# Loads in the order K, Q, V, one octet's Q in five uneven transfers, and a last store in two halves: a linear attention kernel on one core

## The chip, the cores and the metric

The kernel runs on one core of one Trainium2 chip. The time is device microseconds from one launch, as the median of three runs; before the change it is 125.52 us (125.49 to 125.57). The core's work is shared by TensorE (PE in the profile; its weight loads are PEld), VectorE (DVE), ScalarE (ACT), GpSimd (POOL) and SyncE (SP), and by 16 DMA engines that move data between the device memory and the core's SBUF. GpSimd and SyncE issue all transfers here: GpSimd's go through the queue that the profile calls q0 (software_dynamic), SyncE's through q1 (hardware_dynamic).

## The reference

```python
Q_feat = np.maximum(0, Q); K_feat = np.maximum(0, K)      # (8, 12, 512, 64) each
KV    = np.einsum('bhkd,bhkv->bhdv', K_feat, V)
K_sum = np.sum(K_feat, axis=2)
numerator   = np.einsum('bhqd,bhdv->bhqv', Q_feat, KV)
denominator = np.einsum('bhqd,bhd->bhq', Q_feat, K_sum)
out = numerator / (denominator[:, :, :, None] + 1e-10)    # float32
```

There are 96 heads of 512 rows of 64 numbers. For each head a 64 by 64 matrix KV and a vector of 64 sums come from K and V; each row of Q is then multiplied with them. Q, K and V are 12.58 MB each in float32, and so is the output.

## The kernel before, in words

The 96 heads are worked off in 12 octets of eight heads. An octet of Q, K, V or of the output is 1 MB of device memory, seen as 128 rows of 8 KB: row p lies on partition p of a tile, 2048 numbers long. GpSimd's loads change float32 to bfloat16 on the way, so a load reads 1 MB and writes 0.5 MB.

Python code records the order of all instructions. `do.op` (line 58) records one instruction for an engine, works out from what it reads and writes which semaphores it has to wait for, and gives it one to raise. For a transfer this semaphore is a "lane": GpSimd's transfers take six lanes in turn (`LANES`, line 120), and a transfer also waits for the earlier one of its own lane, so at most six of GpSimd's are under way. An engine takes its instructions strictly in the recorded order; a transfer raises its semaphore by 16 when its last part has landed.

The order of the transfers:

- K and V of octet 0 come through SyncE as float32 into two of the seven output tiles `o_sb` (`NOUT`, line 119); Q of octet 0 comes through GpSimd.
- Octets 1 to 9 are loaded ahead (`AHEAD`, line 117) by `load(o)` (line 179): K, V, then Q. Nine tiles each of `q_sb`, `k_sb` and `v_sb` hold them. Octets 10 and 11 are loaded by `step` after the stores of octets 0 and 1, which GpSimd issues too. The last octet, 11, has K, Q, V.
- The stores of octets 2 to 11 (`store`, line 246) are issued by SyncE. All ten list K of octet 11 among what they read (line 253), so the first of them waits until that load has landed; SyncE issues them in order.

The computation, `step(i)` (line 313), is recorded for DVE, ACT and the DMA queues, and runs as a loop over PE in `products` (line 350). For octet i: DVE copies Q (`copy_q`, line 205), PE transposes it into `ps_qt` (line 360) and ACT applies the relu into `qt`; DVE writes relu(K) into `kf` (line 191), DVE and ACT write V into `vo` (lines 200 and 202), PE multiplies the two into `ps_kv` (line 369), ACT moves the result into `kvd` (line 217). Then PE makes the denominators and the eight heads' numerators (line 354), ACT copies these to `ot` (line 225), PE transposes them back into `ps_x` (line 378), and DVE multiplies by the reciprocals (`norm`, line 239, instruction in line 242), in two halves of 16 rows each, into `o_sb` number (o + 2) mod 7. The transposes back, `norm` and `store` of octet o are recorded in step o + 1, between the parts of the next octet. `norm` of octet o writes the tile that `store` of octet o - 7 reads, so it waits until that store has landed: `norm(9)` for `store(2)`, `norm(10)` for `store(3)`, `norm(11)` for `store(4)`.

Of the kernel before, what the change touches and what calls it, by code (L numbers as in the profile page):

```python
# [8 lines left out]
class Order:  # L9
# [45 lines left out]
        for k in writes:  # L55
            self.writer[k], self.readers[k] = (what, n), []

    def op(self, who, make, reads=(), writes=(), sem=None, dma=None, kept=False):
        engine = self.engines[who]
        waits = []  # L60
        assert not self.kept & set(writes)
        if kept:
            self.kept |= set(reads)
        elif dma:
            writes = [*writes, dma]
        todo = self.needs(who, reads, writes)
        while todo:
            x = max(todo, key=lambda y: sum(self.at[y, todo[y]].get(z, 0) >= m for z, m in todo.items()))
            waits.append(self.done[x, todo[x]])
            self.learn(who, x, todo[x])  # L70
            todo = self.needs(who, reads, writes)
        for s, value in waits[:-1]:
            engine.wait_ge(self.sems[s], value)
        made = make(engine)
        if waits:
            s, value = waits[-1]
            made.wait_op(self.sems[s], value, "sem-ge")
        if kept:
            made.then_inc(self.sems[dma], 16)
            self.count[dma] = self.count.get(dma, 0) + 16  # L80
        elif dma:
            made.then_inc(self.sems[dma], 16)
            self.note(who, dma, reads, writes, dma, 16)
        else:
            made.then_inc(self.sems[sem or who], 1)
            self.note(who, who, reads, writes, sem or who, 1)
# [10 lines left out]
def kernel(  # L97
# [8 lines left out]
    B, H, S, D = Q.shape  # L106
    assert D == 64
    P = 128
# [4 lines left out]
    RQ = S * 8 // P  # L113
    U = RQ // 2
    NO = NH // 8
    assert NO * 8 == NH and R == 16 and RQ == 32
    AHEAD = 9
    NI = AHEAD
    NOUT = 7
    LANES = 6  # L120

    fp32 = mybir.dt.float32
    bf16 = mybir.dt.bfloat16
    Act = mybir.ActivationFunctionType
# [2 lines left out]
    sb = ctx.enter_context(tc.tile_pool(name="sb", bufs=1))  # L127
    psum = ctx.enter_context(tc.tile_pool(name="psum", bufs=1, space=bass.MemoryType.PSUM))

    def view(X, f):  # L130
        return X.rearrange("b h s d -> (b h s d)").rearrange("(n p f) -> n p f", p=P, f=f)

    Qr, Kr, Vr, Or = [view(X, RQ * D) for X in (Q, K, V, out)]
# [9 lines left out]
    q2 = sb.tile([P, U, P], bf16, name="q2")  # L143
# [2 lines left out]
    own = sb.tile([P, U, 8, 2], fp32, name="own")  # L146
    den = sb.tile([P, RQ], fp32, name="den")
    rec = sb.tile([P, RQ], fp32, name="rec")
    q_sb = [sb.tile([P, U, P], bf16, name=f"q_sb{i}") for i in range(NI)]
    k_sb = [sb.tile([P, RQ * D], bf16, name=f"k_sb{i}") for i in range(NI)]  # L150
    v_sb = [sb.tile([P, RQ * D], bf16, name=f"v_sb{i}") for i in range(NI)]
    o_sb = [sb.tile([P, RQ, D], fp32, name=f"o_sb{i}") for i in range(NOUT)]
# [3 lines left out]
    ps_x = [psum.tile([P, 1024], fp32, name=f"ps_x{j}") for j in range(2)]  # L156

    names = ["dve", "act", "pool", "pe", "q2", "a0", "d0", "d1", "ev", "t0", "t1", "n0", "n1"]
    lanes = {"pool": [f"gl{i}" for i in range(LANES)], "sp": [f"sl{i}" for i in range(3)], "last": ["el"]}
    sems = {n: tc.alloc_semaphore("s_" + n) for n in names + sum(lanes.values(), [])}  # L160
    turn = {n: 0 for n in lanes}

    def lane(who):
        turn[who] += 1
        return lanes[who][(turn[who] - 1) % len(lanes[who])]

    do = Order(nc, sems)
# [4 lines left out]
        return [(x[o % NI].rearrange("p (r d) -> p r d", d=D), (n, o % NI)) for n, x in (("k", k_sb), ("v", v_sb))]  # L172

    def load_q(o):
        do.op("pool", lambda e: e.dma_start(out=q_sb[o % NI].rearrange("p u f -> p (u f)"), in_=Qr[o],  # L175
                                            single_packet=True),
              writes=[("q", o % NI)], dma=lane("pool"))

    def load(o):
        i = o % NI  # L180
        for n, X, t in (("K", Kr, k_sb), ("V", Vr, v_sb)):
            if n == "V" and o == NO - 1:
                load_q(o)
            do.op("pool", lambda e: e.dma_start(out=t[i], in_=X[o], single_packet=True), writes=[(n.lower(), i)],  # L184
                  dma=lane("pool"))
        if o < NO - 1:
            load_q(o)

    def prep_k(o, s):
        src, key = kv_src(o)[0]  # L190
# [12 lines left out]
        do.op(who, make, reads=[key, ("mask", 1), "vo1"], writes=[("vo", t, j) for j in halves], sem=sem)  # L203

    def copy_q(o):
        do.op("dve", lambda e: e.tensor_copy(q2, q_sb[o % NI]), reads=[("q", o % NI)], writes=["q2"], sem="q2")  # L206

    def relu_q(j):
        do.op("act", lambda e: e.activation(qt[:, j * (U // 2):(j + 1) * (U // 2)], ps_qt[j], Act.Relu),  # L209
              reads=[("pq", j)], writes=[("qt", j)])  # L210
# [3 lines left out]
    def evac_kv():  # L214
        for s in range(2):
            for c in range(2):
                do.op("act", lambda e: e.copy(  # L217
                    kvd[64 * c:64 * c + 64, s:8:2, c * D1:c * D1 + D1].rearrange("p (g t) d -> p g t d", t=2),
                    ps_kv[64 * s:64 * s + 64, :, 0:2 * (D + 2)].rearrange(
                        "p g (t d) -> p g t d", t=2)[:, :, :, c:c + D1]),  # L220
                    reads=[("pk", 0), ("pk", 1)], writes=[("kvd", s, c)], sem="ev" if s + c == 2 else None)
# [21 lines left out]
                                               rec[:, rs].unsqueeze(2).to_broadcast([P, 16, D]), op=Alu.mult),  # L243
              reads=[("x", j), "rec"], writes=[("o", i, j)] if i > 1 else [("o", i, j), ("o", i)], sem=f"n{j}")

    def store(o):
        i = (o + 2) % NOUT
        to, src = Or[o], o_sb[i].rearrange("p r d -> p (r d)")
        keys = [("o", i, h) for h in range(2)]
        if o + AHEAD + 1 < NO:  # L250
            do.op("pool", lambda e: e.dma_start(out=to, in_=src, single_packet=True), reads=keys, dma=lane("pool"))
        else:
            keys.append(("k", (NO - 1) % NI))
            do.op("sp", lambda e: e.dma_start(out=to, in_=src), reads=keys,
                  dma=lane("sp" if o + NOUT < NO else "last"), kept=o + NOUT >= NO)
# [6 lines left out]
    def memset(who, ap, value, key):  # L262
        do.op(who, lambda e: e.memset(ap, value), writes=[key] if isinstance(key, (str, tuple)) else key)  # L263

    def body():
        for c, X in enumerate((Kr, Vr)):
            do.op("sp", lambda e: e.dma_start(out=o_sb[c].rearrange("p r d -> p (r d)"), in_=X[0]),
                  writes=[("o", c)], dma=lane("sp"))
        load_q(0)
        memset("pool", ident, 0.0, "ident")  # L270
        do.op("pool", lambda e: e.affine_select(out=ident, in_=ident, compare_op=Alu.not_equal, fill=1.0, base=0,
                                                pattern=[[-1, P]], channel_multiplier=1),
              reads=["ident"], writes=["ident"])
        ones = vo[:, :, :, 1:D4 - 1]
        memset("pool", ones[:, :, :, 0:D + 2:D1], 0.0, "vo1")
        for h in range(4):
            memset("pool", ones[32 * h:32 * h + 32, :, h % 2, 0:D + 2:D1], 1.0, "vo1")
        for h in range(4):
            for t in range(2):
                memset("pool", mask[32 * h:32 * h + 32, 1, t:t + 1], 1.0 if h % 2 == t else 0.0,  # L280
                       [("m", h, t), ("mask", 1)])
        for o in range(1, AHEAD + 1):
            load(o)
            if o == 1:
                setup()
        for o in range(NO + 1):
            step(o)
        for n in lanes["pool"] + lanes["sp"]:
            nc.gpsimd.wait_ge(sems[n], do.count[n])
        nc.gpsimd.drain()  # L290

# [21 lines left out]
    def step(i):  # L313
        r = i + 1
        more, last = i + 1 < NO, i == NO

        if not last:
            do.looped([("q2", r)], ["q2", "ident"], [("pq", 0)])
            do.looped([], ["q2", "ident"], [("pq", 1)])
            relu_q(0)  # L320
            relu_q(1)
            do.looped([("a0", r), ("d0", r)], KF[0], PK + ["pd"])
            do.looped([("d1", r)], KF[1], PK + ["pd"])
            evac_kv()
            if more:
                prep_v(i + 1, 1, (0,), "act", "a0")
                copy_q(i + 1)
                prep_k(i + 1, 0)
                prep_k(i + 1, 1)
        if i > 0:  # L330
            o = i - 1
            do.looped([("t0", r), ("t1", r)], [*OT, "ident32"], [("x", 0)])
            do.looped([], [*OT, "ident32"], [("x", 1)])
            for j in range(2):
                norm(o, j)
            store(o)
            if o + AHEAD + 1 < NO:
                load(o + AHEAD + 1)
        if not last:
            do.looped([("ev", r)], [*QT, *KVD], ["pd"])  # L340
            denominators()
            for j in range(2):
                do.looped([(f"n{j}", r)], [*QT, *KVD], [("x", j)])
            copy_ot(0, "act")
            copy_ot(1, "act" if more else "dve")
            if more:
                prep_v(i + 1, 0, (0, 1), "dve", "d0")
                prep_v(i + 1, 1, (1,), "dve", "d1")
# [85 lines left out]
```

## Time and profile before

| What | Value |
|---|---|
| median of three runs | 125.52 us |
| the profiled execution | 125.56 us, of which the span from first to last instruction is 123.7 us |
| busy in the span | PE 85.0 us, DVE 82.4, ACT 78.3, POOL 27.6 |
| queue q0 (GpSimd's transfers) | 5184 packets, 75.8% of the 16 DMA engines' span |
| queue q1 (SyncE's transfers) | 1728 packets, 24.7% |
| device memory | 37.75 MB read, 12.58 MB written |

The page gives the span in 40 slices; the row DMA is the mean busy share of the 16 DMA engines in tenths. A query for stretches of time gives the same share for any window. The chain of waits goes back from the last instruction to what released each step. The trace holds two more kinds of records, from which some numbers below are read: each packet's start, duration, size and queue (not the engine that moved it), and the moments at which a transfer's semaphore was raised, 16 for each transfer, one from each DMA engine. A transfer of 128 rows has 144 packets: 128 rows and 16 small ones, of 4 bytes, that raise the semaphore.

### The profile page before, as it was taken

Reading aid. Unit: us, or ns where it says so; the run is one execution under the profiler, and the core shown is the slowest. Engines: PE = TensorE matmul, PEld = TensorE weight load, DVE = VectorE, ACT = ScalarE, POOL = GpSimd, SP = SyncE. Lnnn points to the kernel's source line nnn. Section 1 sums busy time; section 2 is a strip of 40 time slices with the busy share of each in tenths; the row PEclk is TensorE's granted clock in tenths of the full one; section 3 lists DMA queues with packets and bytes.
Section 4 is the critical chain, followed back from the end, with each engine's and each line's share of the span. In section 5 each row is a group of like instructions: output and inputs, shape, how many; then the busy total and the mean of one; then the engine's idle time right before and its main releaser. Section 6 shows DMA issues by size and latency. Waiting matters only on the chain.

```text
span 123.7 us, 3402 instructions
## 1 busy us (share of the span) xinstructions
PE 85.0 (69%) x1440; PEld 73.5 (59%) x1440; DVE 82.4 (67%) x127; ACT 78.3 (63%) x108; POOL 27.6 (22%) x55
## 2 busy tenths in 40 slices
PE   0000097697896979969799697996978918983900
PEld 0000096686794867949589485794856916972900
DVE  1261904769789697895987959869688649067330
ACT  0000762998987889878898788987869736652000
POOL 5795311331131213312421142221000000000000
PEclk9999999999999999999999999999999996897555
DMA  3999999999999999999999999999999999999955
GB/s 69 404 315 222 213 215 212 212 212 212 216 215 215 212 212 212 217 215 213 213 215 212 212 212 267 334 215 234 354 217 212 404 424 432 421 421 429 434 238 212
DMA packets 6916, 32.55 MB, mean 263 GB/s; under 512 B 768, under 2 KB 768, under 8 KB 5120
## 3 DMA queue, kind: packets, MB, share of 16 engines
q0 software_dynamic: 5184, 19.93, 75.8%
q1 hardware_dynamic: 1728, 12.58, 24.7%
q14 instruction: 3, 0.02, 0.0%
q8 instruction: 1, 0.02, 0.0%
HBM read 37.75 MB, written 12.58 MB: 407 GB/s over the span
## 4 chain that ended last, share of the span: by engine, by line
DMA 71%; PE 8%; DVE 7%; issue 5%; POOL 4%; POOLq 0%; DVEq 0%; SPq 0%
DMA k_sb<-in_K_dram 54%; DMA q_sb<-in_Q_dram 12%; DMA out_dram<-o_sb 6%; DVE o_sb L242 5%; PE ps_x L378 4%; PE ps_kv L369 2%; POOL vo L263 2%; PE ps_qt L360 1%; DVE ot_sb L225 1%; PE ps_x L354 1%; POOL k_sb L184 1%; POOL mask L263 1%; POOL q_sb L175 1%; POOL v_sb L184 0%; DVE den L234 0%
## 5 line engine op out<-in xcount | busy, mean ns | idle before, releaser
L242 DVE TENSOR_TENSOR o_sb<-ps_x,rec 128x1024 f32<-128x1024 f32 x24 | 28.5, 1217 | 9.2 <-PE ps_x L378 6.6
L225 ACT COPY ot_sb<-ps_x 128x1024 f32<-128x1024 f32 x23 | 23.2, 1013 | 10.7 <-PE ps_x L354 9.8
L369 PE MATMUL ps_kv<-vo,kf 64*128 64x132 bf16 x768 | 26.7, 228 | 0.8 <-DVE vo L202 0.2
L378 PE MATMUL ps_x<-ident,ot_sb 128*128 128x128 f32 x192 | 25.3, 288 | 1.7 <-DVE ot_sb L225 1.7
L369 PEld LDWEIGHTS ps_kv<-vo,kf 64*128 64x128 bf16 x768 | 24.7, 99 | 2.6 <-issue 2.6
L360 PE MATMUL ps_qt<-ident,q 128*128 128x128 bf16 x192 | 14.4, 235 | 16.4 <-DVE q L206 15.4
L209 ACT ACTIVATE qt<-ps_qt 128x1024 bf16<-128x1024 bf16 x24 | 23.4, 1031 | 1.9 <-PE ps_qt L360 1.9
L378 PEld LDWEIGHTS ps_x<-ident,ot_sb 128*128 128x128 f32 x192 | 22.3, 148 | 3.2 <-issue 2.0
L360 PEld LDWEIGHTS ps_qt<-ident,q 128*128 128x128 bf16 x192 | 12.4, 106 | 19.0 <-DVE q L206 15.4
L217 ACT CAST kvd<-ps_kv 64x260 bf16<-64x260 f32 x48 | 17.9, 374 | 8.5 <-PE ps_kv L369 7.6
L354 PE MATMUL ps_x<-qt,kvd 128*128 128x256 bf16 x96 | 14.9, 281 | 12.1 <-DVE o_sb L242 12.0
L191 DVE TENSOR_SCALAR kf<-k_sb,mask 128x2048 bf16<-128x2048 bf16 x22 | 15.6, 750 | 8.5 <-PE ps_kv L369 8.4
L354 PEld LDWEIGHTS ps_x<-qt,kvd 128*128 128x128 bf16 x96 | 7.7, 100 | 16.9 <-DVE o_sb L242 16.3
L206 DVE COPY q<-q_sb 128x2048 bf16<-128x2048 bf16 x12 | 8.2, 686 | 8.6 <-DMA q_sb<-in_Q_dram 8.6
L175 POOL DMA_DIRECT2D q_sb<-in_Q_dram x12 | 9.2, 763 | 19.0 <-DMA q_sb<-in_Q_dram 14.6
L200 ACT ACTIVATE vo<-v_sb,mask 128x1024 bf16<-128x1024 bf16 x11 | 12.7, 1153 | 0.6 <-DMA v_sb<-in_V_dram 0.4
L202 DVE TENSOR_SCALAR vo<-v_sb,mask 128x2048 bf16<-128x2048 bf16 (+1 forms) x22 | 11.6, 568 | 0.0
L184 POOL DMA_DIRECT2D k_sb<-in_K_dram x11 | 7.7, 697 | 16.8 <-DMA k_sb<-in_K_dram 12.9
L184 POOL DMA_DIRECT2D v_sb<-in_V_dram x11 | 6.3, 576 | 16.5 <-DMA v_sb<-in_V_dram 12.7
L200 ACT ACT_TABLE_LOAD x1 | 1.3, 1283 | 12.2 <-DMA o_sb<-in_V_dram 12.2
L354 PE MATMUL ps_kv<-kvd,qt 128*128 128x16 bf16 x192 | 6.9, 179 | 1.7 <-ACT kvd L217 1.7
L354 PEld LDWEIGHTS ps_kv<-kvd,qt 128*128 128x128 bf16 x192 | 6.4, 96 | 2.0 <-ACT kvd L217 1.9
(21 smaller groups left out, 27.6 us busy)
## 6 DMA issues: line engine op xcount, KB each, us to landing
out_dram<-o_sb SPq DMA_DIRECT2D x10, 1024.0 KB, 12.4
q_sb<-in_Q_dram POOLq DMA_DIRECT2D x12, 512.0 KB, 14.5
k_sb<-in_K_dram POOLq DMA_DIRECT2D x11, 512.0 KB, 14.4
v_sb<-in_V_dram POOLq DMA_DIRECT2D x11, 512.0 KB, 14.4
out_dram<-o_sb POOLq DMA_DIRECT2D x2, 1024.0 KB, 14.7
o_sb<-in_K_dram SPq DMA_DIRECT2D x1, 1024.0 KB, 6.2
o_sb<-in_V_dram SPq DMA_DIRECT2D x1, 1024.0 KB, 10.7
```

Of the source, the lines that this page charges most:

```text
L184: do.op("pool", lambda e: e.dma_start(out=t[i], in_=X[o], single_packet=True), writes=[(n.lower(), i)], dma=lane("pool"))
L191: do.op("dve", lambda e: e.tensor_scalar(kf[:, :, s, :], src, scalar1=0.0, scalar2=mask[:, 0, s:s + 1], op0=Alu.max, op1=Alu.mult), reads= ...
L200: make = lambda e: e.activation(to, src, Act.Copy, scale=m)
L202: make = lambda e: e.tensor_scalar(to, src, scalar1=m, scalar2=None, op0=Alu.mult)
L209: do.op("act", lambda e: e.activation(qt[:, j * (U // 2):(j + 1) * (U // 2)], ps_qt[j], Act.Relu), reads=[("pq", j)], writes=[("qt", j)])
L217: do.op("act", lambda e: e.copy(kvd[64 * c:64 * c + 64, s:8:2, c * D1:c * D1 + D1].rearrange("p (g t) d -> p g t d", t=2), ps_kv[64 * s:64 ...
L225: do.op(who, lambda e: e.copy(to, src) if who == "act" else e.tensor_copy(to, src), reads=[("x", j)], writes=[("ot", j)], sem=f"t{j}")
L242: do.op("dve", lambda e: e.tensor_tensor(o_sb[i][:, rs], ps_x[j].rearrange("p (r d) -> p r d", d=D), rec[:, rs].unsqueeze(2).to_broadcast( ...
L354: return pe.matmul(out_, lhsT, rhs, start=True, stop=True, skip_group_check=True)
L360: x = pe.transpose(ps_qt[u // 8][:, u % 8, :], q2[:, u, :], ident)
L369: x = pe.matmul(ps_kv[:, h, 0:2 * (D + 2)].rearrange("p (t d) -> p t d", t=2), kf[ps, R * g + k, :, :].rearrange("p s d -> p (s d)"), vo[p ...
L378: x = pe.transpose(ps_x[u // 8][:, u % 8 * P:u % 8 * P + P], ot[:, u].rearrange("p h c -> p (h c)"), ident32)
```

## The change

Three things, and the bookkeeping for them.

1. `load(o)` issues K, Q, V for every octet; before, only octet 11 had this order.
2. Q of octet 6, the seventh, is issued as five transfers one after the other, of 40, 11, 45, 7 and 25 rows: partitions 0-39, 40-50, 51-95, 96-102 and 103-127. The five share a semaphore of their own ("arc"). Only the last of the five is noted as the writer of the tile, with the full count of 80; none of the five waits for one of the six lanes, so the lanes of all later transfers of GpSimd move by one.
3. `store` of octet 11 is two transfers on SyncE, each for 16 of a partition's 32 output rows, 4 KB per partition: the first waits for the first `norm` of that octet, the second for the other.

```diff
-        if kept:
+        if kept or more:
             made.then_inc(self.sems[dma], 16)
             self.count[dma] = self.count.get(dma, 0) + 16
...
+    ARCS_AT = 6
+    ARCS = (40, 11, 45, 7, 25)
...
-    q_sb = [sb.tile([P, U, P], bf16, name=f"q_sb{i}") for i in range(NI)]
+    q_sb = [sb.tile([P, RQ * D], bf16, name=f"q_sb{i}") for i in range(NI)]
...
     def load_q(o):
+        if o == ARCS_AT:
+            p = 0
+            for n in ARCS:
+                rows = slice(p, p + n)
+                p += n
+                do.op("pool", lambda e: e.dma_start(out=q_sb[o % NI][rows], in_=Qr[o][rows], single_packet=True),
+                      writes=[("q", o % NI)], dma="arc", more=p < P)
+            return
...
-            if n == "V" and o == NO - 1:
+            if n == "V":
                 load_q(o)
...
-        if o < NO - 1:
-            load_q(o)
...
-    def store(o):
+    def store(o, j=None):
         i = (o + 2) % NOUT
-        to, src = Or[o], o_sb[i].rearrange("p r d -> p (r d)")
-        keys = [("o", i, h) for h in range(2)]
+        rs = slice(0, RQ) if j is None else slice(16 * j, 16 * j + 16)
+        to, src = Or[o].rearrange("p (r d) -> p r d", d=D)[:, rs], o_sb[i][:, rs]
+        keys = [("o", i, h) for h in range(2) if j in (None, h)]
...
             for j in range(2):
                 norm(o, j)
-            store(o)
+                if o == NO - 1:
+                    store(o, j)
+            if o < NO - 1:
+                store(o)
```

More of the change, by code (lines that the diff above doesn't have):

```diff
@@ L56, in note, with op @@
             self.writer[k], self.readers[k] = (what, n), []
-    def op(self, who, make, reads=(), writes=(), sem=None, dma=None, kept=False):
+    def op(self, who, make, reads=(), writes=(), sem=None, dma=None, kept=False, more=False):
         engine = self.engines[who]
@@ L158 @@
     names = ["dve", "act", "pool", "pe", "q2", "a0", "d0", "d1", "ev", "t0", "t1", "n0", "n1"]
-    lanes = {"pool": [f"gl{i}" for i in range(LANES)], "sp": [f"sl{i}" for i in range(3)], "last": ["el"]}
+    lanes = {"pool": [f"gl{i}" for i in range(LANES)], "sp": [f"sl{i}" for i in range(3)], "last": ["el"],
+             "arc": ["arc"]}
     sems = {n: tc.alloc_semaphore("s_" + n) for n in names + sum(lanes.values(), [])}
@@ L174, in load_q @@
     def load_q(o):
-        do.op("pool", lambda e: e.dma_start(out=q_sb[o % NI].rearrange("p u f -> p (u f)"), in_=Qr[o],
-                                            single_packet=True),
+        if o == ARCS_AT:
[6 more added lines that the diff above has]
+            return
+        do.op("pool", lambda e: e.dma_start(out=q_sb[o % NI], in_=Qr[o], single_packet=True),
               writes=[("q", o % NI)], dma=lane("pool"))
@@ L205, in copy_q @@
     def copy_q(o):
-        do.op("dve", lambda e: e.tensor_copy(q2, q_sb[o % NI]), reads=[("q", o % NI)], writes=["q2"], sem="q2")
+        do.op("dve", lambda e: e.tensor_copy(q2.rearrange("p u f -> p (u f)"), q_sb[o % NI]), reads=[("q", o % NI)],
+              writes=["q2"], sem="q2")
     def relu_q(j):
@@ L287, in body @@
             step(o)
-        for n in lanes["pool"] + lanes["sp"]:
+        for n in lanes["pool"] + lanes["arc"] + lanes["sp"]:
             nc.gpsimd.wait_ge(sems[n], do.count[n])
```

## The prediction

> **What bounds the kernel now.** I read the page's row of DMA shares first, then the windows of the last stretch, the chain of waits, and last the packet and landing records of single transfers.
>
> ```profile
> DMA  3999999999999999999999999999999999999955
> GB/s 69 404 315 222 213 215 212 212 212 212 216 215 215 212 212 212 217 215 213 213 215 212 212 212 267 334 215 234 354 217 212 404 424 432 421 421 429 434 238 212
> ```
>
> All slices but the first and the last two are full. The DMA engines work without a pause from 2 us to 118 us: loads (read in float32, counted here as the half that they write), then stores from 96 us on. The end, in windows (columns: window, length, PE, PEld, DVE, ACT, POOL, clock, DMA share, GB/s):
>
> ```profile
> 96.00:118.00 22.00, 16.24 (x216) 14.03 (x210) 12.39 (x18) 9.78 (x15) 0.00 (x0) 0.81 1.01 424
> 118.00:118.50 0.50, 0.00 (x0) 0.00 (x0) 0.50 (x1) 0.00 (x0) 0.00 (x0) 0.50 0.52 213
> 118.50:119.00 0.50, 0.00 (x0) 0.00 (x0) 0.41 (x1) 0.00 (x0) 0.00 (x0) 0.50 0.12 49
> 119.00:119.50 0.50, 0.00 (x0) 0.00 (x0) 0.00 (x0) 0.00 (x0) 0.00 (x0) 0.50 0.16 66
> 119.50:120.00 0.50, 0.00 (x0) 0.00 (x0) 0.00 (x0) 0.00 (x0) 0.00 (x0) 0.50 0.66 279
> 120.00:122.00 2.00, 0.00 (x0) 0.00 (x0) 0.00 (x0) 0.00 (x0) 0.00 (x0) 0.50 1.05 442
> ```
>
> From 118.5 to 119.5 us the share is 0.12 to 0.16, which is two engines of 16. They are still at the store of octet 10 while the others are idle. The chain of waits:
>
> ```profile
> 14.54 14.43 DMA k_sb<-in_K_dram
> 28.96 0.28 issue
> 29.25 14.50 DMA k_sb<-in_K_dram
> 43.74 0.28 issue
> 44.03 14.43 DMA k_sb<-in_K_dram
> ...
> 93.27 7.43 DMA out_dram<-o_sb
> 100.70 0.02 issue
> 100.72 2.37 DVE o_sb L242 x2
> ...
> 117.68 1.23 DVE o_sb L242
> ```
>
> The loads follow one another: from 14.54 to 44.03 us GpSimd issues 12, so one takes 2.46 us, and one of an engine's eight rows 0.307 us. The chain then goes through `store(2)`, whose landing at 100.70 us lets `norm(9)` begin, and 18.2 us of computation to the last `norm`, done at 118.91 us. In the packet records the last store's first rows start at 119.77 us, its last ends at 122.40; the semaphore is full at 122.75.
>
> That chain hides the real bound. Of `store(2)`'s 16 landings the first is at 98.84 us, fifteen have come by 99.67 and the last comes at 100.70: one DMA engine, A, is late. It is late in every transfer (1.4 us behind the first at 40 us, 1.8 at 100), since a 16 KB packet of an instruction queue took 0.94 us of it at 4.77 us; nothing lets it catch up. In the packet records A raises the semaphore of `store(10)` at 119.945 us and starts on the last store at 119.951: it never rests, and it ends the kernel. The next, B, is done with `store(10)` at 119.68 us; then come engines at 118.82, 118.77 and 118.65, and the rest by 118.46. So the time is A's total work, with B 0.26 us behind it; the computation had 0.18 us left.
>
> **The change, part by part.**
>
> Five transfers in place of one. 128 rows divide evenly over 16 engines, eight each; 40, 11, 45, 7 and 25 do not. No transfer of the trace shows how such rows are spread, so the effect on A's eight rows of this load is bounded by none left (8 x 0.307 = 2.46 us gained) and, below nothing, by one engine receiving a whole transfer, the largest being 45 rows ((45 - 8) x 0.307 = 11.4 us lost). I take the spread by which the counts come out even: 40 = 10 engines x 4 rows, 11 x 1, 15 x 3, 7 x 1, 5 x 5, each transfer starting at the engine after the one before. 10 + 11 + 15 + 7 + 5 = 48 is three turns of 16. From the first engine, place 0, on: places 0 to 3 get 4 + 1 + 3 = 8 rows, place 4 gets 4 + 1 + 1 = 6, places 5 to 9 get 4 + 3 + 1 = 8, place 10 gets 1 + 3 + 1 = 5, places 11 to 15 get 1 + 3 + 5 = 9. Place 10 is relieved by three rows, 0.92 us, place 4 by two, 0.61 us; five places carry 0.31 us more. The Trainium skill ("DMA: Bandwidth & Descriptors", "Why a DMA increments its semaphore by 16 and not by 1") states this spread: the largest number of engines up to 16 that divides the rows, consecutive from a cursor that goes round; it adds that GpSimd gives some copies to all 16, rows divided by 16 and rounded up, which is a rival below. No trace so far shows either.
>
> Where A stands: in the very first transfer the engines start one after another, and the stream that later holds the 16 KB packet starts at 2.104 us, 0.119 us after the first. In the last transfer the landings follow at 12 ns (0.182 us over 15). 0.119 / 0.012 is place 10, an estimate good to one place or two, if engines are started in their order and the circle begins at place 0. I take A as relieved by three rows and B by two, which nothing but the forecast's likelihood rests on.
>
> The new landings: each of the five transfers also has 16 completion packets, four more per engine than before; on this queue such a packet takes 22 ns and the next row follows its start after 12 to 21, so 0.05 to 0.09 us; I take 0.07.
>
> The end, then. A is done with `store(10)` at 119.945 - 0.92 + 0.07 = 119.10 us, B at 119.68 - 0.61 + 0.07 = 119.14, and the third engine, with a row more, at 118.82 + 0.31 + 0.07 = 119.20. That one is last: 0.75 us earlier than A was.
>
> The last store in halves. Its sixteen 4 KB packets per engine replace eight of 8 KB. No such packet is in the trace: half of an 8 KB row's 0.309 us each is a cost of nothing, and a full 0.309 each is 2.47 us. The 4-byte packets take 9 ns, and a line from there to 8 KB at 0.309 gives 0.159 each, 0.07 us in all, which I take: bytes set the duration in both rows. The gain on the late engines is nothing in itself, as they come to the last store only at 119.1 us. What it does is to keep them fed: the first half is issued after the first `norm` (117.27 us), starts 0.86 us later as the last store did now (118.91 to 119.77), so at 118.1, before any late engine needs it. The first half lasts eight packets, 1.27 us, so until 120.4 us, and the second is there by 119.77 even if the computation ends as now. With one store, an unmoved computation would have held the gain at 0.18 us.
>
> The computation should move as well: `norm(9)` waits for `store(2)`, where A lands 0.85 us earlier and the next of the sixteen landings are 1.0 us before A's (99.67), or 0.38 later than that with a row more (100.05). So it begins 0.65 to 0.85 us earlier. I count nothing for it, as the halves give 0.6 us of room behind it.
>
> The order K, Q, V. Each Q comes one load (2.46 us) earlier, each V one later; the number of bytes ahead of the last K and behind it is the same, so SyncE's stores are released as before. Q's waits on DVE (8.6 us in seven waits) go or shrink. V is then the late one: for octet 10 it lands at 88.3 us where ACT first takes it at 90.64, for octet 1 at 19.1 us where ACT is free near 21. Should that cover go, ACT's copy is late and `ps_kv` of the next octet with it, up to 2.46 us, but before 96 us the stores wait for loads anyway, and after octet 10 the order is the old one. Count: nothing.
>
> GpSimd issues five times instead of once. A load's issue takes 0.53 us; five full ones would be 2.1 us more. GpSimd sits idle 1.5 to 2.0 us before each issue, waiting for a lane, and a load lands 14.5 us after its issue behind five others, so the queue does not run dry. The loads queued behind the five (V of octet 6 first) are issued up to 2.1 us later at worst and still land in their turn: nothing. The fifth wait added to GpSimd's last waits, for the arc semaphore, is long met. SyncE issues one store more, 0.5 us, while the late engines still work: nothing.
>
> Sum, against the profiled execution: 125.56 - 0.75 + 0.07 = 124.88; the median lies 0.04 us below that execution, so 124.84 us.
>
> **The rivals.** About 0.2% (0.25 us) is what a measurement can tell from no change.
>
> *The circle misses the late engines.* Nine of 16 places keep eight rows. Then A stays as it is plus 0.07 and 0.07: 125.66 us. The same holds if A is relieved but B is not (119.68 + 0.14, so 125.4), or if rows come out even after all. For it: the place of A is an estimate, that of B unknown, since the streams nearly coincide in phase. Against it: A's start.
>
> *The late engine gets a ninth row* (the slower side). Place 11 is the neighbour of my estimate. Then A has 0.31 + 0.14 more and 125.97 us follows; it decides as soon as A stands at places 11 to 15. B there would be at 119.68 + 0.31 + 0.14, 0.19 us beyond A now, 125.7 us. The Trainium skill ("DMA: Bandwidth & Descriptors", "Latency and other measured facts") has engines 7 and 15 as the usually slower ones; by it A at 15 would be this rival, A at 7 the one before. The trace has one persistently late engine up to 50 us, not two, and shows a cause for it: 0.02 of this rival's chance is for that rule.
>
> *Each transfer is dealt from the first engine on*, 3, 1, 3, 1 and 2 rows each: places 0 to 6 get ten rows, 7 to 10 nine, 11 eight, 12 seven, 13 four, 14 three, 15 none. A at place 10 has a row more, 125.97 us; among the first seven 126.27; at 12 or beyond it is relieved, and B or an engine with 0.61 us more is last, near 125.1 to 125.4.
>
> *The 4 KB packets are dear.* At the upper bound, 2.4 us more, it would be slower at 127.2 us whatever the rows do; the two sizes seen follow bytes, so this has little weight.
>
> **How the numbers follow.** Both late engines relieved 0.61, with 124.84 us and its own range of 124.5 to 125.15 (the halves free and A last, down to 124.7, and 0.2 for the computation; dear completions upward). Missed 0.17: 125.4 to 125.8. A ninth row 0.11: 125.7 to 126.0. Dealt from the first 0.09: 0.05 of it slower. Dear packets 0.02. Faster by over 0.2% (under 125.27 us): 0.61 and 0.03 from the fourth case, 0.64. Within 0.2%: 0.14 of the misses and 0.01 of the rest, 0.15. Slower: 0.21. The range from 124.5 to 125.8 leaves out the slower cases and little below.
>
> **What would show it.** After: landings of every transfer behind octet 6's Q with the last of 16 about 0.9 us behind the first instead of 1.4; `store(2)` landing near 99.9 us; in the windows from 118 to 119.2 us no long stretch with two engines; the last packets ending near 121.7. Wrong if the last landing still trails by 1.4 us or more, if other engines take A's place, or if the last store's packets pause.

## The result, and the profile after

The changed kernel takes 126.03 us (125.93 to 126.13, six runs) against 125.47 us (125.38 to 125.57, six runs) before: a ratio of 1.0038, 95% interval 1.0024 to 1.0053. It is slower by about half a microsecond (0.48 us by the ratio, 0.56 by the medians), where 124.84 us had been forecast, and it lies outside the range. The profiled execution took 125.94 us with a span of 124.1 us.

The same rows of the page as before, and the queue of GpSimd:

```profile
DMA  2999999999999999999999999999999999999991
GB/s 90 387 306 227 213 214 213 215 214 217 211 213 211 214 214 213 210 214 213 215 214 215 213 214 281 310 215 251 342 215 234 408 420 422 420 428 428 413 383 44
...
q0 software_dynamic: 5280, 19.93, 75.7%
```

The last but one slice is now full and the last nearly empty, where both had been half full. The end in windows (columns as in the prediction):

```profile
118.50:119.00 0.50, 0.00 (x0) 0.00 (x0) 0.00 (x0) 0.00 (x0) 0.00 (x0) 1.00 0.94 385
119.00:119.50 0.50, 0.00 (x0) 0.00 (x0) 0.00 (x0) 0.00 (x0) 0.00 (x0) 1.00 0.97 401
119.50:120.00 0.50, 0.00 (x0) 0.00 (x0) 0.00 (x0) 0.00 (x0) 0.00 (x0) 0.86 1.04 426
120.00:122.00 2.00, 0.00 (x0) 0.00 (x0) 0.00 (x0) 0.00 (x0) 0.00 (x0) 0.50 0.53 217
122.00:122.50 0.50, 0.00 (x0) 0.00 (x0) 0.00 (x0) 0.00 (x0) 0.00 (x0) 0.50 0.12 49
122.50:123.00 0.50, 0.00 (x0) 0.00 (x0) 0.00 (x0) 0.00 (x0) 0.00 (x0) 0.50 0.02 8
```

The gap of 118.5 to 119.5 us is closed: the halves keep the engines busy. But the engines now stop one by one from 120 us on, and after 122 us only two of 16 still work. The rows moved are the same; they are spread worse. In the landing records the last engine trails the first by 4.0 to 4.1 us in every load behind octet 6's Q but the very last, which overlaps the first stores (2.0 us just ahead of octet 6's Q), where the forecast had 0.9. The chain of waits at its end:

```profile
93.59 7.45 DMA out_dram<-o_sb
101.04 0.02 issue
101.07 2.37 DVE o_sb L253 x2
...
114.11 1.08 PE ps_x L393 x8
115.19 0.03 issue
115.22 0.02 DVEq L73
115.24 0.04 issue
115.28 2.36 DVE o_sb L253 x2
```

The computation ended at 117.64 us, 1.27 us earlier than in the profile of before, mainly because the last transposes ran at the full granted clock (1.00 in place of 0.50 from 114 us on), and the kernel was slower all the same. The computation is not the bound here.

The two profiles alone can't size the loss. In the one after, the late engine A was 0.35 us later from the first transfer on (last landing 7.46 us against 7.11; its 16 KB packet came at 5.13 us against 4.77), and still 0.35 us later at K of octet 6, just ahead of the five transfers (its packet that raises the semaphore: 51.128 us against 50.778). That is how two executions differ; the sizes below come from the times of all runs.

**How the rows were really spread.** The packet records show it. Sorted into streams by the regular distance of an engine's packets (0.305 us from row to row, about 0.02 us after a small packet), the packets between K of octet 6 and V of octet 6 form sequences like these (rows, then R for the packet that raises the semaphore, p for another packet of 4 bytes):

```
3R 1R 3R 1R 2R          places 0 to 6      10 rows
3R 1R 3R pR 2R          places 7 to 10      9 rows
...
pppR pR pppR pR ppR     place 15            0 rows
```

This is the rival "dealt from the first engine on": the rows divided by 16 and rounded up (3, 1, 3, 1, 2) to each engine in turn, until they run out, beginning anew with each transfer. What is short is filled up with packets of 4 bytes, and that can be counted on the page. The five transfers have 48 + 16 + 48 + 16 + 32 = 160 places for 128 rows, so 32 fillers, and 64 more semaphore packets: 5184 + 96 = 5280, the number in the row above, against this row of before:

```profile
q0 software_dynamic: 5184, 19.93, 75.8%
```

The Trainium skill ("DMA: Bandwidth & Descriptors", "Why a DMA increments its semaphore by 16 and not by 1") names both spreads; here the one that it gives as the exception for GpSimd holds, and its circle does not occur.

A's own stream fits best with nine rows: from its raise for K to its raise for V of octet 6 it took 51.128 to 56.417 us, 5.29 us, for which two even loads need 4.91. With 0.375 us more it got a row and the small packets.

### The profile page after: what moved, and what is told of

Same layout as the page of the kernel before. It is cut to its first block, busy times and chain, and to the rows that moved or that the text cites. A ratio compares the mean times of both kernels' runs of the same rounds, so it can differ in the third digit from the quotient of the medians.

```text
span 124.1 us, 3408 instructions
## 1 busy us (share of the span) xinstructions
PE 84.5 (68%) x1440; PEld 73.2 (59%) x1440; DVE 82.0 (66%) x127; ACT 78.5 (63%) x108; POOL 28.8 (23%) x59
## 3 DMA queue, kind: packets, MB, share of 16 engines
q0 software_dynamic: 5280, 19.93, 75.7%
## 4 chain that ended last, share of the span: by engine, by line
DMA 73%; DVE 7%; PE 6%; issue 4%; POOL 4%; POOLq 0%; DVEq 0%; SPq 0%
DMA k_sb<-in_K_dram 42%; DMA q_sb<-in_Q_dram 14%; DMA v_sb<-in_V_dram 12%; DMA out_dram<-o_sb 6%; DVE o_sb L253 6%; PE ps_x L393 2%; PE ps_kv L384 2%; POOL vo L275 2%; PE ps_qt L375 1%; POOL q_sb L188 1%; DVE ot_sb L236 1%; PE ps_x L369 1%; POOL mask L275 1%; DVE den L245 0%; DVE rec L248 0%
## 5 line engine op out<-in xcount | busy, mean ns | idle before, releaser
L384 PE MATMUL ps_kv<-vo,kf 64*128 64x132 bf16 x768 | 27.2, 230 | 0.6
L384 PEld LDWEIGHTS ps_kv<-vo,kf 64*128 64x128 bf16 x768 | 25.3, 100 | 2.5 <-issue 2.5
L375 PE MATMUL ps_qt<-ident,q 128*128 128x128 bf16 x192 | 15.1, 241 | 16.7 <-DVE q L216 15.8
L393 PE MATMUL ps_x<-ident,ot_sb 128*128 128x128 f32 x192 | 23.6, 276 | 1.7 <-DVE ot_sb L236 1.7
L375 PEld LDWEIGHTS ps_qt<-ident,q 128*128 128x128 bf16 x192 | 13.0, 109 | 19.3 <-DVE q L216 15.8
L393 PEld LDWEIGHTS ps_x<-ident,ot_sb 128*128 128x128 f32 x192 | 20.8, 140 | 3.2 <-issue 2.0
L188 POOL DMA_DIRECT2D q_sb<-in_Q_dram x11 | 7.3, 660 | 15.5 <-DMA q_sb<-in_Q_dram 6.7
```

What stands on the lines that cost most here:

```text
L375: x = pe.transpose(ps_qt[u // 8][:, u % 8, :], q2[:, u, :], ident)
L384: x = pe.matmul(ps_kv[:, h, 0:2 * (D + 2)].rearrange("p (t d) -> p t d", t=2), kf[ps, R * g + k, :, :].rearrange("p s d -> p (s d)"), vo[p ...
L393: x = pe.transpose(ps_x[u // 8][:, u % 8 * P:u % 8 * P + P], ot[:, u].rearrange("p h c -> p (h c)"), ident32)
```

## The experiments

All of them are compared with the kernel before on the same chip in the same hour; intervals are 95%. A loss in us is the ratio's share of the time before; it can differ from the difference of the two medians by 0.1 us or so.

**One part alone.** The five transfers alone (`load_q` as in the change; the order of the loads and `store` as before):

> The kernel before with Q of octet 6 in the five transfers of 40, 11, 45, 7 and 25 rows, and nothing else changed. Theory: the packets of the changed kernel show each transfer dealt out from the first engine on, its rows divided by 16 and rounded up per engine (3, 1, 3, 1 and 2), so that the late engine A, which fits places 7 to 10, carries nine rows in place of eight; that is 0.31 us and 0.07 to 0.1 us for eight more small packets, so 0.3 to 0.45 us slower than before. Rival one: the order K, Q, V is what costs, then this run is within 0.1 us of before. Rival two: the two half stores are, with the same result here.

Measured: 125.97 us against 125.61, ratio 1.0042 (1.0018 to 1.0067), a loss of 0.53 us like that of the whole change.

The order of the loads alone:

```diff
-            if n == "V" and o == NO - 1:
+            if n == "V":
                 load_q(o)
...
-        if o < NO - 1:
-            load_q(o)
```

> The kernel before with K, Q, V in every octet and nothing else. Theory: nothing, within 0.1 us of before, since the bytes ahead of and behind the last K are the same and DMA engine A never rests. Rival: the later V holds up ACT and the steps, 0.3 us or more slower.

Measured: 125.60 us, ratio 1.0003 (0.9979 to 1.0027). The two half stores alone (`store(o, j)` after each `norm` of the last octet, as in the change's diff):

> The kernel before with the last octet's output in two half stores and nothing else. Theory: engine A comes to the last store at the same time as before and moves sixteen packets of 0.159 us in place of eight of 0.309 us: 0 to 0.1 us slower. Rival: the second store and its packets cost more, 0.3 us or more slower. A gain of over 0.2 us would mean that the computation and not A sets the end.

Measured: 125.59 us, ratio 1.000 (0.998 to 1.0021). So the whole loss comes with the five transfers. The order does what it says to the waits: DVE's wait for Q is gone but for one, and the wait moves to `kf`, the tile of relu(K), which PE still reads. The lines of the waits of before, and then of the order alone:

```profile
DVE q L206 <- DMA q_sb<-in_Q_dram: 8.6, 7, 3.8
DVE kf L191 <- PE ps_kv L369: 8.4, 9, 1.3
```

```profile
DVE kf L200 <- PE ps_kv L380: 14.8, 11, 2.2
DVE q L215 <- DMA q_sb<-in_Q_dram: 0.3, 1, 0.3
```

(Columns: total us, number of times, longest.) In this profile `store(2)` lands at 100.93 us against 100.70, as much later as A's first load (7.34 against 7.11), so the order moved nothing else there, and the median stays. The profiled execution itself took 126.48 us: its computation ended at 119.84 us, and the last store, in one piece, waited for it. With one store the computation is close behind the DMA engines, as the prediction's 0.18 us of room said.

**The cut at place ten.** Other rows in the same five transfers, chosen so that the place of A can be read:

```diff
-    ARCS = (40, 11, 45, 7, 25)
+    ARCS = (96, 10, 9, 8, 5)
```

> The changed kernel with other rows in the five transfers: 96, 10, 9, 8 and 5. Dealt out from the first engine this gives ten rows to places 0 to 4, nine to 5 to 7, eight to place 8, seven to place 9 and six to places 10 to 15. If A is at place 10, the run is 0.61 - 0.1 - 0.05, so about 0.45 us faster than before, or less if an engine with ten rows becomes the last; at place 9 about 0.15 us faster, at 8 0.15 us slower, at 7 0.45 us slower. If A were not among places 7 to 10, or the rows went round in a circle, the time would not follow this list: a circle has 16, 10, 9, 8 and 5 engines, and gives each place eight, nine or seven rows from the four small ones wherever it begins after the even 96.

Measured: 126.00 us, ratio 1.0036 (1.0018 to 1.0053). By the list this reads as "A at place 7", but the records say otherwise: A's stream took 51.032 to 55.383 us over Q and V, 4.35 us, 0.56 less than two even loads, and only six rows fit that (places 10 to 15): its six rows of the first transfer are followed by that transfer's raise at 52.881 us, and its first row of V starts at 52.947, which leaves 0.066 us, room for small packets and for no row. Nine rows in the change leave places 7 to 10. The one place in both lists is 10. So A was relieved by two rows, and the kernel became slower. The landings of the stores say who took A's place: from 101.1 to 115.8 us the last of the 16 falls from 1.68 to 2.46 us behind the first, while the second to last stays at 1.67. This is the second late engine of the kernel before (the prediction's B, called C from here on), which fell back from 0.85 to 1.66 us behind in the same stretch there. The sum by the times of before: C was done with the store of octet 10 at 119.68 us, A at 119.95. Two rows and 0.07 us put C at 120.36, 0.41 beyond A; with 0.07 for the halves 0.48 us, and 0.45 were measured (interval 0.23 to 0.67). That places C among 0 to 4.

**The splitting or the rows.** The same number of transfers, but even ones, and two uneven transfers instead of five:

```diff
-    ARCS = (40, 11, 45, 7, 25)
+    ARCS = (32, 16, 32, 16, 32)
```

> The changed kernel with 32, 16, 32, 16 and 32 rows in the five transfers: as many transfers and semaphore raises, but each engine has eight rows again. Theory: the row that engine A has more is what costs, so this run is 0 to 0.15 us slower than before (four more completion packets and the halves) and 0.3 us faster than the change. Rival: the splitting itself costs (issue, completion packets, the order of the landings), then it is 0.3 to 0.5 us slower than before, like the change.

Measured: 125.55 us against 125.46, ratio 1.0002 (0.999 to 1.0013). The five even transfers cost nothing that can be measured. The uneven pair:

```diff
-    ARCS = (40, 11, 45, 7, 25)
+    ARCS = (88, 40)
```

> The changed kernel with Q of octet 6 in two transfers only, of 88 and 40 rows. Dealt out from the first engine: nine rows on places 0 to 12, seven on 13, four on 14, none on 15. Theory: A at place 10 has a row more as in the change, with three fewer transfers: 0.3 to 0.4 us slower than before. Rival of the splitting: a quarter of the change's loss, about 0.1 us.

Measured: 125.78 us, ratio 1.0021 (1.001 to 1.0033), 0.26 us with an interval of 0.13 to 0.41. This is nearer to the row than to a quarter of the loss, but the interval is too wide to call it exact. The counts of GpSimd's packets agree with the filling-up in both. The row of the even five (64 more raises, no filler):

```profile
q0 software_dynamic: 5248, 19.93, 75.9%
```

and that of the two uneven (16 raises, 144 - 128 = 16 fillers):

```profile
q0 software_dynamic: 5216, 19.93, 75.8%
```

**The dose.** The five uneven transfers in two octets, each with a semaphore of its own:

```diff
-    ARCS_AT = 6
+    ARCS_AT = (5, 6)
...
-        if o == ARCS_AT:
+        if o in ARCS_AT:
...
-                      writes=[("q", o % NI)], dma="arc", more=p < P)
+                      writes=[("q", o % NI)], dma=f"arc{o}", more=p < P)
```

> The changed kernel with the five uneven transfers for Q of octet 5 as well as of octet 6. Theory: A has two rows more, and the loss doubles to 0.7 to 0.85 us. If the loss came once, from a start or from a wait and not from A's rows, it stays at about 0.4 us.

Measured: 126.65 us, ratio 1.0093 (1.0075 to 1.011): 1.17 us, more than the 0.7 to 0.85 expected. The loss does come with each octet, so it is no matter of a start or a single wait; but the expectation counted A's two rows alone. C, among the first places, gets two rows per octet: 119.68 + 4 x 0.305 + 0.14 = 121.04 us, 1.10 beyond A's 119.945, and 0.07 for the halves makes 1.17. This was worked out after the run; A alone would give 0.82. The packet records of this run agree with it: C's last raise comes at 123.29 us, A's at 122.91.

The page's windows of this kernel show the longer tail, from nearly all 16 engines at 120.5 to 121 us down to two:

```profile
120.50:121.00 0.50, 0.00 (x0) 0.00 (x0) 0.00 (x0) 0.00 (x0) 0.00 (x0) 0.50 0.98 401
121.00:121.50 0.50, 0.00 (x0) 0.00 (x0) 0.00 (x0) 0.00 (x0) 0.00 (x0) 0.50 0.88 361
121.50:122.00 0.50, 0.00 (x0) 0.00 (x0) 0.00 (x0) 0.00 (x0) 0.00 (x0) 0.50 0.54 221
122.00:122.50 0.50, 0.00 (x0) 0.00 (x0) 0.00 (x0) 0.00 (x0) 0.00 (x0) 0.50 0.32 131
122.50:123.00 0.50, 0.00 (x0) 0.00 (x0) 0.00 (x0) 0.00 (x0) 0.00 (x0) 0.50 0.12 49
```

**A relieved, C with one row.**

```diff
-    ARCS = (40, 11, 45, 7, 25)
+    ARCS = (96, 10, 10, 10, 2)
```

> The changed kernel with 96, 10, 10, 10 and 2 rows: ten rows on places 0 and 1, nine on 2 to 9, six on 10 to 15. A at place 10 has two rows fewer. If A alone set the end, 0.45 us faster than before. Theory after the cut at ten: a second late engine, C, 0.26 us behind A before, stands among the first places and takes the lead as soon as it gets a row; then 0.05 to 0.2 us slower than before if C has one row more (places 2 to 9), and 0.45 us slower if it has two (0 or 1), as in the cut at ten.

Measured: 125.66 us, ratio 1.0013 (1.0001 to 1.0025): 0.16 us slower. A had its two rows fewer (51.104 to 55.454 us over Q and V, 4.35 us again; its landings trail by about 1.4 us in place of 1.9), and the kernel gained nothing, since one engine falls back during the stores from 1.25 us at 98.6 us to 2.12 at 115.8. With one row the sum puts C at 0.18 us beyond the time of before. Against the cut at ten, where C had two rows, 0.29 us are saved, about the row's 0.305, though each of the two numbers is uncertain by 0.15 to 0.2 us. The packet records say the same more sharply. C's raises can be followed back from the stores to octet 6's Q. In the cut at ten C took 0.69 us longer over Q and V than two even loads, as the engines with ten rows did there; here it took 0.375 us longer, as those with nine rows did. So C is among places 2 to 4.

No version that beats both came of this. In all these runs dealing begins at the first engine, so what is taken from place 10 goes to the places ahead of it, C's too. With A 0.26 us behind C and 0.6 of a row to the first ten places for each row taken from the last six, the two would be level at an estimated 0.26 / 1.6 = 0.16 us earlier than A was, before the extra packets' 0.1. What is left is less than can be measured, and rows are whole.

## Why the prediction was wrong

**The step that failed is the spread of the uneven rows**, "I take the spread by which the counts come out even". It was a choice among readings that the trace of before could not tell apart, made because 10 + 11 + 15 + 7 + 5 happens to be three turns of 16. By it A was to lose three rows, 0.92 us, and B two; instead A's stream got one row more (0.375 us with the small packets), and C, the prediction's B, two by its place. The rival, dealing from the first engine with rounding up, had a chance of 0.09; it is what happens, in the packet sequences and in the packet counts of the change and of all six kernels with split loads. The number that this rival gave for "A at place 10", 125.97 us, is the measured 126.03 to 0.06; that closeness is partly luck, since it counts A alone. The range ended at 125.8 us, short of it.

**A's place was right.** Start order in the first transfer gave place 10; the change's stream leaves 7 to 10, the cut leaves 10 to 15.

**That DMA engines end the kernel was right, that A alone does was half right.** With uneven rows the kernel is 0.48 us slower; with both octets, 1.17; with five even transfers, nothing. But the sum for the one row of A is 0.31 + 0.07 + 0.07 = 0.45, and for C with two rows -0.26 + 0.61 + 0.07 + 0.07 = 0.49. Which of the two ends the changed kernel is left open: they are 0.04 us apart. The profiles show that it varies. By the last raise A is last in the profile of the change (122.80 us, C 122.36), but it was 0.35 us late there from the first transfer on; C is last in the profile of the even five (122.30, A 122.22), where both have eight rows. The prediction saw C only as an engine to be relieved, "B by two", and had no case in which it gets two rows more; every run that relieved A was stopped by it. The rival of the missed circle did say that a relief of A without B gains little.

**The rest of the sum held.** The 4 KB packets take 0.159 us each, as the line through two sizes gave, and the half stores alone change nothing (ratio 1.000). The order K, Q, V costs and brings nothing that can be measured (ratio 1.0003). GpSimd needs 2.53 us to issue the five transfers, the worst case of the prediction, and nobody waits for it:

```profile
36.97 1.04 POOL L196 DMA_DIRECT2D k_sb<-in_K_dram  x1 [1.64 <-DMA k_sb<-in_K_dram]
38.00 2.53 POOL L185 DMA_DIRECT2D q_sb<-in_Q_dram  x5
40.52 0.55 POOL L196 DMA_DIRECT2D v_sb<-in_V_dram  x1
41.94 0.54 POOL L196 DMA_DIRECT2D k_sb<-in_K_dram  x1 [0.87 <-DMA v_sb<-in_V_dram]
```

GpSimd is idle again, for 0.87 us, two issues later. "A never rests" and the room behind the computation were right too: the computation ended 1.27 us earlier without effect.

**What would have changed the forecast.** The four kinds of outcome were all listed. The weights were not earned: for the circle spoke no row of this case, and where no row tells two spreads apart, nearly even weights would have put the middle of the forecast at no gain.

## What to carry to other kernels

When all DMA engines are busy from start to end, as here, the end belongs to the one engine that runs latest, and the mean share hides it: read the spread of the 16 landings of each transfer, and follow more than the last one. A GpSimd load of this kind whose row count is no multiple of 16 loaded the first engines and spared the last ones, every time anew; five odd transfers don't average out, they add up. Before relieving one late engine, look at how far the next is behind it: here it was 0.26 us in the profile of before, 0.40 with the halves alone and nothing in the even five, where C is 0.07 us behind A.

## What was not expected of the hardware

The fillers: a short share is made up with 4-byte packets to the full count, so that the packet count of a queue tells how a transfer was dealt.

The 16 KB packet at about 5 us is there in every profile, 0.93 to 0.94 us long, and the last landing of the first transfer trails by 1.7 to 2.5 us in each; A's lag at octet 6 differs from execution to execution, 1.3 to 2.2 us.

Not all of A's lag comes from that packet. In the kernel before, a single row of 0.70 us in place of 0.32 at 86.1 us put A back by another 0.37, so the 1.8 us of the prediction are 1.4 and this row; the even five and the halves alone have no such row of A. The 8 KB packets of an instruction queue at 52.3 and 53.8 us there, 0.32 us each, fall in the load in which two other engines dropped back by 0.3 to 0.5 us each. Such single events are as large as the row that was dealt wrong, so one profile can't rank two engines that are 0.3 us apart.

C falls back steadily only during the stores. Single rows, of 8 KB, take 0.33 to 0.40 us in place of 0.309, most of them between about 104 and 111 us, in the kernel before as in the cut at ten and the order alone; C's raises of two stores come up to 2.78 us apart there, those of the others 2.45. Nothing in these runs tells why; it was not tried.
